# Diagonal and neighbour level of the recurrent heads as split elementwise products, and a paced recurrence

## The chip, the cores and the metric

The kernel runs on one core of one Trainium2 chip. The core has a matrix engine (TensorE, PE in the rows; its weight loads are PEld), a vector engine (DVE), an activation engine (ACT), a general engine (POOL) and a queue engine (SP), and sixteen DMA engines that move data between memory and the core. The metric is the device time of one execution in microseconds (us), lower is better.

## The reference

The program is one layer of an encoder over 512 positions of width 1024, in float32: a token mixer (eight-head grouped attention with axial rotary positions, beside four heads of a bidirectional gated recurrence), a cross-attention into 256 memory rows, and a gated feed-forward with a short convolution. The change lies in the recurrence. For one head and one direction it computes

```
b     = cumsum(log f)                                   # per key channel, f in (lb, 1)
o[t]  = sum over s <= t, channels c, of  q[t,c] * k[s,c] * exp(b[t,c] - b[s,c]) * v[s]
k     = 1 - f
```

and the backward direction is the same on the flipped sequence. Both are summed, so position t meets every position s once through a decay of one direction, and itself twice (k forward plus k backward, no decay).

## The kernel before

Everything is laid out with 128 channels on the partitions and 512 positions along the free axis. A large product in float32 is made of three matmuls on halves: each operand is split into a rounded part in the reduced type float32r and its remainder, and `mm3` (lines 277 to 280) multiplies high by high, high by low and low by high. A weight unit of 128x1024 is loaded, cast by ACT (line 222) and completed by DVE, or by ACT and a summing DMA (lines 224 to 230).

The recurrence of one head is `hgrn_core` (line 618). It has no chunks in time. It builds the 128x128 blocks of the score matrix by levels: level m (1, 2, 4, ... 64) fills the entries whose positions lie in neighbouring runs of m inside a pair of runs. `qk` holds queries and keys of both directions, already multiplied with the decays inside the runs; a level takes the keys (copied to `kc`) and the queries, multiplies them on TensorE in plain float32 (line 647, four 128x128 matmuls into one bank `ps_c`), and DVE merges the result into `diag` through a mask (line 679, `copy_predicated`). Then DVE multiplies the queries and keys with the decay to the next run in place (line 673, two instructions) and the run decays with each other (line 678). The diagonal itself is a product of its own ahead of the levels: `ksum`, the key sum of both directions (lines 628 and 629), times q (line 636), copied to `diag` by ACT (line 637). Level 1 pairs each position with its neighbour and uses copies `kc` and `qc` (line 632). Levels 128 and 256 cross the blocks (lines 654 to 666), and lines 685 to 687 apply the scores to v. Each plain float32 matmul shows as two records in the trace, so a group of four as x8.

Heads 0 to 2 run beside the input projections: `weave` (line 73) steps two generators, `mix_projections` (gate, head 1, head 2, queries of the attention, head 3, keys and values) and `cores`, and always advances the one whose done share of its given total is smaller. A projection step is six wide matmuls and counts 1.296, a level counts 1.0; the totals are 100 and 53 (`CORE_SHARE`). Head h can begin when its inputs are projected. Head 3 runs in a second `weave` beside the attention and a filler of projections. The order in which the generators emit instructions is their rank: the framework (Tile) then places each engine's instructions by that rank, by what is ready in its own plan, and by free buffers, and each engine runs its list strictly in that order. `rope_q` and `turn_q` (lines 770 to 784) rotate the attention's queries on DVE, ACT and TensorE while head 3 is projected; they read the projection's banks `ps_s` and `ps_o`, which the keys and values need next.

Temporary buffers have tags; `th` has four buffers (`kc`, `qc`, `ksum` and others), `tq` three. The bank `ps_c` has two.

Of the kernel before, what the change touches and what calls it, by code (L numbers as in the profile page):

```python
# [9 lines left out]
F32 = mybir.dt.float32  # L10
F32R = mybir.dt.float32r
# [3 lines left out]
ALU = mybir.AluOpType  # L15
# [3 lines left out]
P = 128  # L19
D = 1024  # L20
T = 512
NB = T // P
# [25 lines left out]
NEG_SCALAR = frozenset(range(9, 33))  # L48
NEG_POOL = frozenset(range(33, 42))
CORE_SHARE, ATT_LEAD = 53.0, 4.0  # L50
KEY_TURNS = {1: (0, 1), 2: (2, 3)}
WARM, SPREAD_STEP = 4, 2
LEVELS = (1, 2, 4, 8, 16, 32, 64)
# [5 lines left out]
def pat(t, off, dims):  # L59
    a = t[:]  # L60
    return bass.AP(tensor=a.tensor, offset=a.offset + off, ap=[list(a.ap[0])] + [list(d) for d in dims])
# [8 lines left out]
        return self.hi[kc // n][:, kc % n, sl], self.lo[kc // n][:, kc % n, sl]  # L70


def weave(*streams):
    live = [[g, 0.0, float(total)] for g, total in streams]
    while live:
        live.sort(key=lambda s: s[1] / s[2])
        for s in live:
            try:
                step = next(s[0])
            except StopIteration:  # L80
                live.remove(s)
                break
            if step is not None:
                s[1] += step
                break
        else:
            raise RuntimeError("no stream can go on")


def layer(tc, io, out):  # L90
    nc = tc.nc
    ctx = ExitStack()
    pool = lambda name, **k: ctx.enter_context(tc.tile_pool(name=name, **k))
    const = pool("const", bufs=1)
# [13 lines left out]
    def bank(tag):  # L108
        return ps.tile([P, 512], F32, name="ps_" + tag, tag=tag)
# [4 lines left out]
    def tmp2(shape=(P, 512), dt=F32, tag="ta"):  # L114
        return t2.tile(list(shape), dt, name="tmp2", tag=tag, bufs=TMP_BUFS[tag])
# [4 lines left out]
    def split(hi, lo, src, eng=None):  # L120
        nc.scalar.copy(hi, src)  # L121
        (eng or nc.vector).tensor_sub(lo, src, hi.bitcast(F32))  # L122
# [159 lines left out]
    def blk(b):  # L282
        return slice(b * P, (b + 1) * P)
# [153 lines left out]

    ident = const.tile([P, P], F32, name="ident")
    gcol = const.tile([P, KC], F32, name="gcol")
    ones = const.tile([P, P], F32, name="ones")  # L440
    nhalf = const.tile([P, 16], F32, name="nhalf")
    mark = const.tile([P, 1], F32, name="mark")
    warm = tmp2()
    xt = [big([P, 4, T]) for _ in range(2)]
    nc.scalar.dma_start(gcol, io["gx"])
    nc.gpsimd.memset(ones, 1.0)
    nc.vector.memset(warm[:, :256], 0.0)
    nc.gpsimd.memset(nhalf, -0.5)
# [44 lines left out]
    for j in range(4):  # L493
# [8 lines left out]
        for k in range(2):  # L502
            kc = 2 * j + k
            for a, w in ((0, wh), (0, wl), (1, wh)):
                for b in range(NB):
                    nc.tensor.matmul(v_ps[b], hT.get(kc, blk(b))[a], w[:, half(k)],
                                     start=kc == 0 and a == 0 and w is wh, stop=kc == 7 and a == 1)
# [2 lines left out]
        nc.sync.dma_start(xr[b], io["x"][blk(b), :])  # L510
    ident_r = const.tile([P, P], F32R, name="ident_r")
    nc.vector.tensor_copy(ident_r, ident)
    issued[0] = taken[0] = 4
    hold[0] = 6
    issue_ahead()
# [22 lines left out]
    masks = const.tile([P, len(LEVELS), P], U8, name="masks")  # L538
# [79 lines left out]
    def hgrn_core(h):  # L618
        while h not in heads:
            yield None  # L620
        q, qk, tt = heads[h]
        room = big([P, 2048])
        a = room[:, 0:1024].rearrange("p (s w n) -> p s w n", s=NB, w=2)
        kt = room[:, 1024:1536].rearrange("p (s n) -> p s n", s=NB)
        st = room[:, 1536:1792].rearrange("p (g n) -> p g n", g=2)
        diag = a[:, :, 0, :]
        ksum, kc, qc = [tmp2(tag="th") for _ in range(3)]
        nc.scalar.mul(ksum, qk[:, 1, 0, :], oml[:, 0, h:h + 1])
        nc.vector.scalar_tensor_tensor(out=ksum, in0=qk[:, 1, 1, :], scalar=oml[:, 1, h:h + 1], in1=ksum,
                                       op0=ALU.mult, op1=ALU.add)  # L630
        for side, to in ((1, kc), (0, qc)):
            (nc.vector.tensor_copy if (h, side) == (1, 0) else nc.scalar.copy)(
                to, pat(qk, side * 2 * T, [[2, T // 2], [T + 1, 2]]))
        o = bank("c").rearrange("p (b n) -> p b n", b=NB)
        for b in range(NB):
            nc.tensor.matmul(o[:, b, :], ksum[:, blk(b)], q[:, blk(b)], start=True, stop=True)
        nc.scalar.copy(diag, o)
        yield 1.0
        toff = 0
        for i, m in enumerate(LEVELS + (128, 256)):  # L640
            if m <= 64:
                if m > 1:
                    kc = tmp2(tag="th")
                    nc.scalar.copy(kc, pat(qk, 2 * T, [[2 * m, T // (2 * m)], [T + m, 2], [1, m]]))
                o = bank("c").rearrange("p (b n) -> p b n", b=NB)
                for b in range(NB):
                    nc.tensor.matmul(o[:, b, :], kc[:, blk(b)], qc[:, blk(b)] if m == 1 else  # L647
                                     pat(qk, b * P, [[2 * m, P // (2 * m)], [T + m, 2], [1, m]]),
                                     start=True, stop=True)
            elif m == 128:  # L650
                o = bank("c").rearrange("p (b n) -> p b n", b=NB)
                for sb in range(NB):
                    tb = sb ^ 1
                    nc.tensor.matmul(o[:, sb, :], qk[:, 1, sb % 2, blk(sb)], qk[:, 0, tb % 2, blk(tb)],
                                     start=True, stop=True)
            else:
                o = bank("c").rearrange("p (b n) -> p b n", b=NB)
                for sb in range(NB):
                    nc.tensor.transpose(o[:, sb, :], qk[:, 1, sb // 2, blk(sb)], ident)
                nc.scalar.copy(kt, o)  # L660
                yield 0.5
                o = bank("c")[:, :256].rearrange("p (g n) -> p g n", g=2)
                for sb in range(NB):
                    nc.tensor.matmul(o[:, sb // 2, :], kt[:, sb, :], v[:, sb, blk(h)],
                                     start=sb % 2 == 0, stop=sb % 2 == 1)
                nc.scalar.copy(st, o)
                yield 1.0
                break
            nblk = T // m
            npair = nblk // 2  # L670
            for s, off, gap in ((1, 1, nblk - 1), (0, nblk + 1, -(nblk + 1))):
                c = pat(qk, s * 2 * T, [[2 * m, npair], [T + m, 2], [1, m]])
                nc.vector.tensor_tensor(out=c, in0=c, in1=pat(tt, toff + off, [[2, npair], [gap, 2], [0, m]]),  # L673
                                        op=ALU.mult)
            if m < 128:
                src = tt[:, toff:toff + 2 * nblk].rearrange("p (i two) -> p two i", two=2)
                toff += 2 * nblk
                nc.vector.tensor_mul(tt[:, toff:toff + nblk], src[:, 0, :], src[:, 1, :])
                nc.vector.copy_predicated(diag, masks[:, i:i + 1, :].to_broadcast([P, NB, P]), o)
            else:  # L680
                nc.scalar.copy(a[:, :, 1, :], o)
            yield 1.0
        o = bank("c").rearrange("p (b n) -> p b n", b=NB)
        for tb in range(NB):
            nc.tensor.matmul(o[:, tb, :], a[:, tb, 0, :], v[:, tb, blk(h)], start=True, stop=False)
            nc.tensor.matmul(o[:, tb, :], a[:, tb ^ 1, 1, :], v[:, tb ^ 1, blk(h)], start=False, stop=False)
            nc.tensor.matmul(o[:, tb, :], qk[:, 0, tb // 2, blk(tb)], st[:, 1 - tb // 2, :], start=False, stop=True)
        on = tmp2((P, NB, P), tag="th")
        ss = small()
        for b in range(NB):  # L690
            nc.scalar.activation(on[:, b, :], o[:, b, :], ACT.Square, accum_out=ss[:, b:b + 1])
        r = rstd_of(ss[:, :NB], NB, P)
        yield 3.0
        while len(sg_box) < 1 + NB:
            yield None
        for b in range(NB):
            nc.vector.scalar_tensor_tensor(out=on[:, b, :], in0=o[:, b, :], scalar=r[:, b:b + 1],
                                           in1=sg_box[0][:, b, blk(h)], op0=ALU.mult, op1=ALU.mult)
        o = bank("c").rearrange("p (b n) -> p b n", b=NB)
        for b in range(NB):  # L700
            nc.tensor.transpose(o[:, b, :], on[:, b, :], ident)
        if h % 2 == 0:
            pair(mix, 2 + h // 2)
        split_scaled(*mix.get(4 + h, slice(0, T)), o.rearrange("p b n -> p (b n)"), og[:, 0:1])
        rec_done[0] += 1
        yield 0.5
# [224 lines left out]
    def attention_filler():  # L931
        kv["k"] = Act([None] * 2, [None] * 2)
        for c in range(8):
# [3 lines left out]
            for step in proj_fm(kv["m"], M, "b", put_kx(c)):  # L937
                yield step
                turned[0] = c > max(KEY_TURNS)
            for b in KEY_TURNS.get(c, ()):  # L940
# [87 lines left out]
    acts, sides, gates, last_act = [], [], {}, [None]  # L1028
# [63 lines left out]
    us = [bank(up_tags[n]) for n in range(4)]  # L1092
# [10 lines left out]
    wide = [big([P, 2, 4, 256]) for _ in range(2)]  # L1103
# [14 lines left out]
    near, far = half_t  # L1118
# [40 lines left out]
    for i in range(2, NF):  # L1159
        if i in UP_S:  # L1160
            strassen_pair(i)
        else:
            for c in range(2):
                o = next_bank()
# [182 lines left out]
```

## Time and profile before

| | |
|---|---|
| time, median of 3 runs | 816.31 us (816.14 to 816.73) |
| profiled execution, first to last instruction | 813.8 us |
| TensorE busy | 803.3 us, 99% |
| weight loads (PEld) busy | 691.0 us, 85% |
| DVE busy | 574.7 us, 71% |
| ACT busy | 482.1 us, 59% |
| POOL busy | 136.9 us, 17% |

The span of the profiled execution counts from its first to its last instruction; the runs' times hold in addition what lies around it, 2.5 us by the median. Busy time of TensorE is the union of its records, whose ends are modelled; distances from start to start are what a matmul really takes of the engine. The granted TensorE clock is full (2.4 GHz) in all forty slices of the span.

### The profile page before, as it was taken

To read this page: it belongs to the slowest core of one execution; us is meant where nothing else is said; L and a number is where in the kernel's file an instruction comes from. 1 tells how busy PE (TensorE), PEld (TensorE's weight loads), DVE (VectorE), ACT (ScalarE), POOL (GpSimd) and SP (SyncE) were. 2 spreads that over 40 slices of the span, in tenths; PEclk is the share of its full clock that TensorE was granted. 3 is DMA by queue.
4 is the path that set the end of the run, shared out by engine and by line. 5 is a ranking of instruction groups with operands and counts; after the bars stand their busy time and mean duration, and the time that the engine had idled before them with its cause. 6 is when DMAs were issued, how large, how long until landed. Compare 5 with 4: busy or idle time off the path is not lost.

```text
span 813.8 us, 11771 instructions
## 1 busy us (share of the span) xinstructions
PE 803.3 (99%) x4426; PEld 691.0 (85%) x4426; DVE 574.7 (71%) x868; ACT 482.1 (59%) x796; POOL 136.9 (17%) x213
## 2 busy tenths in 40 slices
PE   9999999999999999999999999999999999999996
PEld 7888888889998887888888898899999998888885
DVE  5456587469886865855453767987777788888765
ACT  5675757459988874644543553665555545566651
POOL 0111201053233102301010311211111111000301
PEclk9999999999999999999999999999999999999999
DMA  8685645569899753256634158776665677278852
GB/s 296 202 259 139 160 103 117 118 159 247 229 250 254 182 172 126 78 181 157 180 117 142 33 164 208 154 200 166 179 171 143 150 200 178 91 208 278 239 130 104
DMA packets 42457, 139.61 MB, mean 172 GB/s; under 512 B 5280, under 2 KB 6560, under 8 KB 42400
## 3 DMA queue, kind: packets, MB, share of 16 engines
q1 hardware_dynamic: 28944, 97.43, 35.5%
q0 software_dynamic: 12160, 38.54, 26.2%
q10 hardware_dynamic: 1296, 2.89, 1.0%
q8 instruction: 34, 0.56, 0.3%
q14 instruction: 23, 0.19, 0.1%
HBM read 135.17 MB, written 25.17 MB: 197 GB/s over the span
## 4 chain that ended last, share of the span: by engine, by line
PE 92%; DVE 3%; ACT 2%; issue 1%; POOL 1%; DMA 0%; DVEq 0%; POOLq 0%; SPq 0%; ACTq 0%
PE ps_b L279 10%; PE ps_b L280 10%; PE ps_b L278 10%; PE ps_s L278 6%; PE ps_s L280 6%; PE ps_s L279 6%; PE ps_o L278 5%; PE ps_o L279 5%; PE ps_o L280 5%; PE ps_c L278 5%; PE ps_c L280 5%; PE ps_c L279 5%; PE ps_c L647 3%; PE ps_o L893 2%; PE ps_s L872 2%; PE ps_o L882 2%
## 5 line engine op out<-in xcount | busy, mean ns | idle before, releaser
L222 ACT CAST wh<-raw 128x1024 fp32r<-128x1024 f32 x110 | 113.7, 1035 | 114.6 <-PE ps_b L279 35.3
L224 DVE TENSOR_TENSOR wl<-raw,wh 128x1024 fp32r<-128x1024 f32 (+1 forms) x77 | 92.3, 1201 | 72.2 <-ACT wh L222 72.0
L278 PE MATMUL ps_b<-big,wh 128*128 128x512 f32 (+1 forms) x344 | 122.3, 355 | 0.0
L280 PE MATMUL ps_b<-big,wl 128*128 128x512 f32 (+1 forms) x344 | 121.2, 352 | 0.0
L279 PE MATMUL ps_b<-big,wh 128*128 128x512 f32 (+1 forms) x344 | 121.2, 352 | 0.0
L280 PEld LDWEIGHTS ps_b<-big,wl 128*128 128x128 f32 x344 | 65.1, 189 | 8.5 <-DMA wl<-in_wu_dram 0.2
L278 PEld LDWEIGHTS ps_b<-big,wh 128*128 128x128 f32 x344 | 65.1, 189 | 8.3
L279 PEld LDWEIGHTS ps_b<-big,wh 128*128 128x128 f32 x344 | 65.1, 189 | 8.1
L673 DVE TENSOR_TENSOR big<-big 128x512 f32<-128x512 f32 x64 | 47.2, 755 | 9.6 <-PE ps_c L647 4.0
L278 PE MATMUL ps_s<-wh,big 128*128 128x512 f32 (+1 forms) x140 | 53.4, 383 | 0.0
L279 PE MATMUL ps_s<-wl,big 128*128 128x512 f32 (+1 forms) x140 | 53.3, 381 | 0.0
L280 PE MATMUL ps_s<-wh,big 128*128 128x512 f32 (+1 forms) x140 | 53.0, 379 | 0.0
L230 POOL DMA_DIRECT2D wl<-in_w_dram x33 | 29.3, 887 | 126.7 <-ACT wl L229 91.5
L122 DVE TENSOR_TENSOR big<-ps_o,big 128x512 fp32r<-128x512 f32 x54 | 36.9, 687 | 15.0 <-ACT big L121 13.4
L121 ACT CAST big<-ps_o 128x512 fp32r<-128x512 f32 x54 | 31.7, 588 | 18.5 <-PE ps_o L996 7.5
L278 PE MATMUL ps_s<-big,wh 128*128 128x256 f32 (+1 forms) x120 | 40.0, 334 | 0.0
L279 PE MATMUL ps_s<-big,wh 128*128 128x256 f32 (+1 forms) x120 | 40.0, 333 | 0.0
L280 PE MATMUL ps_s<-big,wl 128*128 128x256 f32 (+1 forms) x120 | 40.0, 333 | 0.0
L278 PE MATMUL ps_o<-wh,big 128*128 128x512 f32 (+1 forms) x102 | 39.2, 385 | 0.0
L279 PE MATMUL ps_c<-big,wh 128*128 128x256 f32 (+1 forms) x120 | 39.1, 326 | 0.0
L278 PE MATMUL ps_c<-big,wh 128*128 128x256 f32 (+1 forms) x120 | 39.1, 326 | 0.0
L280 PE MATMUL ps_c<-big,wl 128*128 128x256 f32 (+1 forms) x120 | 39.1, 326 | 0.0
(315 smaller groups left out, 2149.3 us busy)
## 6 DMA issues: line engine op xcount, KB each, us to landing
raw<-in_w_dram SPq DMA_DIRECT2D x91, 512.0 KB, 3.6
wl<-in_w_dram POOLq DMA_DIRECT2D x33, 512.0 KB, 7.3
sum_t<-in_wd_dram SPq DMA_DIRECT2D x20, 512.0 KB, 6.3
tmp<-in_wu_dram SPq DMA_DIRECT2D x14, 512.0 KB, 6.9
sum_t<-in_wd_dram POOLq DMA_DIRECT2D x10, 512.0 KB, 8.4
sum_t<-sum_t POOLq DMA_DIRECT2D x10, 512.0 KB, 7.5
big<-sum_t SPq DMA_DIRECT2D x10, 512.0 KB, 4.7
raw<-sum_t SPq DMA_DIRECT2D x10, 512.0 KB, 4.4
```

What stands on the lines that cost most here:

```text
L121: nc.scalar.copy(hi, src)
L122: (eng or nc.vector).tensor_sub(lo, src, hi.bitcast(F32))
L222: nc.scalar.copy(wh, raw)
L224: last_low[0] = nc.vector.tensor_sub(wl[:, :by_dma], raw[:, :by_dma], wh[:, :by_dma].bitcast(F32)).ins
L230: nc.gpsimd.dma_start(wl[:, by_dma:], source(i)[:, by_dma:], accum_op=ALU.add)
L278: nc.tensor.matmul(o, a[0], b[0], start=start, stop=False, skip_group_check=again)
L279: nc.tensor.matmul(o, a[0], b[1], start=False, stop=False, skip_group_check=again)
L280: last_mm[0] = nc.tensor.matmul(o, a[1], b[0], start=False, stop=stop, skip_group_check=again).ins
L647: nc.tensor.matmul(o[:, b, :], kc[:, blk(b)], qc[:, blk(b)] if m == 1 else pat(qk, b * P, [[2 * m, P // (2 * m)], [T + m, 2], [1, m]]), st ...
L673: nc.vector.tensor_tensor(out=c, in0=c, in1=pat(tt, toff + off, [[2, npair], [gap, 2], [0, m]]), op=ALU.mult)
L872: nc.tensor.matmul(s, qT[h // 4][:, h % 4, blk(qb)], kT[:, 2 * (h // 4) + c, :], start=c == 0, stop=c == 1)
L882: nc.tensor.transpose(o[:, c, :], e[:, 0, blk(c)], ident)
```

## The change

For heads 0 to 2 (`wide`), the diagonal and level 1 are no longer matrix products. DVE multiplies neighbours elementwise (each query with the neighbour's key of the right direction) and `ksum` with q, and interleaves them into two planes of 128x512, `near`: in plane 0 an even column holds the diagonal and an odd column the pair, in plane 1 the other way round. Both planes are split into high and low parts, and four float32r matmuls of 128x512 with a stationary pattern of ones and zeros in alternate columns (`parity`) sum the channels: row s of the result receives plane s mod 2. ACT copies the result to `diag`; entries that are neither diagonal nor pair are overwritten by the later levels. Head 3 keeps the former way, with all its copies on ACT.

In both weaves the recurrence is now paced by a clock that counts what all streams have emitted: after each level it waits until 2.0 of other work has been emitted (`CORE_STEP`), before the pattern products 6.0 (`CORE_WIDE`), before head 3's diagonal 3.0 (`CORE_FIRST`); when nobody else can go on, the wait is dropped. `ones` moves to a temporary buffer, and `parity` takes its place among the constants.

```diff
+CORE_FIRST, CORE_STEP, CORE_WIDE = 3.0, 2.0, 6.0
+clock, stuck = [0.0], [False]
+def pace(us):
+    end = clock[0] + us
+    while clock[0] < end and not stuck[0]:
+        yield None
 def weave(*streams):
...
             if step is not None:
                 s[1] += step
+                clock[0] += step
+                stuck[0] = False
                 break
         else:
-            raise RuntimeError("no stream can go on")
+            if stuck[0]:
+                raise RuntimeError("no stream can go on")
+            stuck[0] = True
...
-    ones = const.tile([P, P], F32, name="ones")
+    parity = const.tile([P, P + 2], F32R, name="parity")
...
+    ones = tmp2((P, P), tag="tq")
...
+    for i in range(2):
+        nc.vector.memset(parity.rearrange("p (i two) -> p i two", two=2)[:, :, i].bitcast(F32), 1.0 - i)
...
-        ksum, kc, qc = [tmp2(tag="th") for _ in range(3)]
+        wide = h < 3
+        near = room[:, 1024:2048]
+        ksum = tmp2(tag="th")
         nc.scalar.mul(ksum, qk[:, 1, 0, :], oml[:, 0, h:h + 1])
+        if wide:
+            nc.vector.tensor_tensor(out=pat(near, T, [[2, T // 2], [1 - T, 2]]), in0=pat(qk, 0, [[2, T // 2], [T + 1, 2]]),
+                                    in1=pat(qk, 3 * T + 1, [[2, T // 2], [-(T + 1), 2]]), op=ALU.mult)
         nc.vector.scalar_tensor_tensor(out=ksum, in0=qk[:, 1, 1, :], scalar=oml[:, 1, h:h + 1], in1=ksum,
                                        op0=ALU.mult, op1=ALU.add)
-        for side, to in ((1, kc), (0, qc)):
-            (nc.vector.tensor_copy if (h, side) == (1, 0) else nc.scalar.copy)(
-                to, pat(qk, side * 2 * T, [[2, T // 2], [T + 1, 2]]))
-        o = bank("c").rearrange("p (b n) -> p b n", b=NB)
-        for b in range(NB):
-            nc.tensor.matmul(o[:, b, :], ksum[:, blk(b)], q[:, blk(b)], start=True, stop=True)
-        nc.scalar.copy(diag, o)
-        yield 1.0
+        if wide:
+            pairs = lambda t: t.rearrange("p (i two) -> p i two", two=2)
+            nc.vector.tensor_tensor(out=pat(near, 0, [[2, T // 2], [T + 1, 2]]), in0=pairs(ksum), in1=pairs(q),
+                                    op=ALU.mult)
+            sides = [[tmp2(dt=F32R, tag="th") for _ in range(2)] for _ in range(2)]
+            for n in range(2):
+                split(*sides[n], near[:, n * T:n * T + T])
+        else:
...
+            yield from pace(CORE_FIRST)
...
-            if m <= 64:
+            if m == 1 and wide:
+                pass
+            elif m <= 64:
...
-                nc.vector.copy_predicated(diag, masks[:, i:i + 1, :].to_broadcast([P, NB, P]), o)
+                if m == 1 and wide:
+                    yield from pace(CORE_WIDE)
+                    o = bank("c")
+                    for n in range(2):
+                        for k in range(2):
+                            nc.tensor.matmul(o, parity[:, n:n + P], sides[n][k], start=n + k == 0, stop=n + k == 2)
+                    nc.scalar.copy(diag, o.rearrange("p (b n) -> p b n", b=NB))
+                else:
+                    nc.vector.copy_predicated(diag, masks[:, i:i + 1, :].to_broadcast([P, NB, P]), o)
             else:
                 nc.scalar.copy(a[:, :, 1, :], o)
             yield 1.0
+            yield from pace(CORE_STEP)
```

## Rows read from the trace of the kernel before

**Rows 1.** The page, first part: each engine's busy time, share, instructions.
```profile
PE 803.3 (99%) x4426; PEld 691.0 (85%) x4426; DVE 574.7 (71%) x868; ACT 482.1 (59%) x796; POOL 136.9 (17%) x213
```

**Rows 2.** Waits of TensorE: total us, times, longest us.
```profile
PE ps_c L647 <- DVE big L673: 0.7, 1, 0.7
...
PE ps_c L647 <- ACT tmp L644: 0.5, 1, 0.5
```

**Rows 3.** Timeline of TensorE, head 0: start, duration, line, tiles, count.
```profile
44.79 0.39 PE L278 MATMUL ps_s<-wh,big 128*128 128x512 f32 x1
...
50.45 0.39 PE L279 MATMUL ps_s<-wl,big 128*128 128x512 f32 x1
...
54.31 1.05 PE L636 MATMUL ps_c<-tmp,tmp 128*128 128x128 f32 x8
55.11 0.48 PE L278 MATMUL ps_o<-wh,big 128*128 128x512 f32 x1
55.43 1.05 PE L647 MATMUL ps_c<-tmp,tmp 128*128 128x128 f32 x8
56.24 0.48 PE L279 MATMUL ps_o<-wl,big 128*128 128x512 f32 x1
```

**Rows 4.** Timeline of head 1 on TensorE, DVE and ACT.
```profile
99.21 1.04 ACT L229 ACTIVATE wl<-wh 128x1024 fp32r<-128x1024 f32 x1
99.34 0.75 DVE L607 SCALAR_TENSOR_TENSOR big<-big,oml,tmp 128x512 f32<-128x512 f32 x1
99.47 1.13 PE L636 MATMUL ps_c<-tmp,tmp 128*128 128x128 f32 x8
100.35 0.48 PE L279 MATMUL ps_b<-big,wh 128*128 128x512 f32 x1
...
100.90 0.40 PE L278 MATMUL ps_b<-big,wh 128*128 128x512 f32 x1
...
101.04 2.15 DVE L673 TENSOR_TENSOR big<-big 128x512 f32<-128x512 f32 x2
101.25 1.13 PE L647 MATMUL ps_c<-tmp,tmp 128*128 128x128 f32 x8
102.14 0.47 PE L279 MATMUL ps_b<-big,wh 128*128 128x512 f32 x1
...
103.33 1.20 PE L647 MATMUL ps_c<-big,tmp 128*128 128x128 f32 x8 [0.72 <-DVE big L673]
```

**Rows 5.** Timeline of TensorE, first groups of head 3.
```profile
195.43 1.06 PE L636 MATMUL ps_c<-tmp,tmp 128*128 128x128 f32 x8
...
207.46 1.16 PE L647 MATMUL ps_c<-big,tmp 128*128 128x128 f32 x8 [0.52 <-ACT tmp L644]
```

**Rows 6.** Single lines: shortest, median, longest duration in ns.
```profile
L679 DVE COPY_PREDICATED big<-masks,ps_c x28: 706/730/751, 56.6 to 236.9; 128x512 f32<-128x512 uint8 x28
...
L121 ACT CAST tmp<-tmp x4: 604/620/627, 177.1 to 191.4; 128x512 fp32r<-128x512 f32 x4
...
L122 DVE TENSOR_TENSOR tmp<-tmp,tmp x4: 681/686/694, 177.9 to 192.3; 128x512 fp32r<-128x512 f32 x4
...
L647 PEld LDWEIGHTS ps_c<-tmp,tmp x32: 187/192/193, 55.2 to 199.9; 128*128 128x128 f32 x32
```

**Rows 7.** Windows: length, busy us (instructions) of each engine, clock, DMA share, GB/s.
```profile
core 0: us, PE busy (x) PEld busy (x) DVE busy (x) ACT busy (x) POOL busy (x), PEclk, DMA share, GB/s
...
165.00:180.00 15.00, 15.00 (x76) 12.60 (x75) 10.50 (x20) 8.93 (x19) 7.61 (x10) 1.00 0.61 131
180.00:196.00 16.00, 16.00 (x137) 15.58 (x136) 15.43 (x28) 14.54 (x25) 6.38 (x8) 1.00 0.91 255
```

**Rows 8.** DVE by line, 130 to 166 us: busy us, mean ns, idle before.
```profile
L673 DVE TENSOR_TENSOR big<-big 128x512 f32<-128x512 f32 x16 | 11.6, 745 | 5.3 <-PE ps_c L654 2.3 <-PE ps_c L647 1.9 <-ACT tmp L644 1.1
L679 DVE COPY_PREDICATED big<-masks,ps_c 128x512 f32<-128x512 uint8 x7 | 5.1, 729 | 0.0
```

**Rows 9.** Timeline, hand-over of the last query bank to keys and values.
```profile
187.41 0.68 DVE L736 TENSOR_TENSOR tmp<-ps_o,big 128x512 f32<-128x512 f32 x1
...
188.38 0.28 PE L278 MATMUL ps_o<-wh,big 128*128 128x256 f32 x1
```

More of the change, by code (lines that the diff above doesn't have):

```diff
@@ L626, in hgrn_core @@
         diag = a[:, :, 0, :]
-        ksum, kc, qc = [tmp2(tag="th") for _ in range(3)]
+        wide = h < 3
+        near = room[:, 1024:2048]
+        ksum = tmp2(tag="th")
         nc.scalar.mul(ksum, qk[:, 1, 0, :], oml[:, 0, h:h + 1])
+        if wide:
+            nc.vector.tensor_tensor(out=pat(near, T, [[2, T // 2], [1 - T, 2]]), in0=pat(qk, 0, [[2, T // 2], [T + 1, 2]]),
+                                    in1=pat(qk, 3 * T + 1, [[2, T // 2], [-(T + 1), 2]]), op=ALU.mult)
         nc.vector.scalar_tensor_tensor(out=ksum, in0=qk[:, 1, 1, :], scalar=oml[:, 1, h:h + 1], in1=ksum,
                                        op0=ALU.mult, op1=ALU.add)
-        for side, to in ((1, kc), (0, qc)):
-            (nc.vector.tensor_copy if (h, side) == (1, 0) else nc.scalar.copy)(
-                to, pat(qk, side * 2 * T, [[2, T // 2], [T + 1, 2]]))
-        o = bank("c").rearrange("p (b n) -> p b n", b=NB)
-        for b in range(NB):
-            nc.tensor.matmul(o[:, b, :], ksum[:, blk(b)], q[:, blk(b)], start=True, stop=True)
-        nc.scalar.copy(diag, o)
-        yield 1.0
+        if wide:
[6 more added lines that the diff above has]
+        else:
+            kc, qc = [tmp2(tag="th") for _ in range(2)]
+            for side, to in ((1, kc), (0, qc)):
+                nc.scalar.copy(to, pat(qk, side * 2 * T, [[2, T // 2], [T + 1, 2]]))
+            yield from pace(CORE_FIRST)
+            o = bank("c").rearrange("p (b n) -> p b n", b=NB)
+            for b in range(NB):
+                nc.tensor.matmul(o[:, b, :], ksum[:, blk(b)], q[:, blk(b)], start=True, stop=True)
+            nc.scalar.copy(diag, o)
+            yield 1.0
         toff = 0
         for i, m in enumerate(LEVELS + (128, 256)):
-            if m <= 64:
+            if m == 1 and wide:
+                pass
+            elif m <= 64:
                 if m > 1:
```

## The prediction

> **What bounds the kernel now.** I read the page's busy times first, then TensorE's waits, then its timeline from start to start, and last the busy times of short windows. The page gives TensorE 803.3 of 813.8 us [rows 1]: the reader is to see that an instruction removed from it shortens the kernel, unless something else comes to the fore. The waits say how little is left to gain by order alone: in the level products (line 647) TensorE waited 0.7 us once for DVE and 0.5 us once for ACT [rows 2]. The first is in head 1, at 103.33 [rows 4]. The second is in head 3, at 207.46 [rows 5]. Because ends of matmuls are modelled, I price TensorE by starts. A wide float32r product of 512 columns takes 0.227 us: from 44.79 to 50.45 lie 25 of them, 5.66 us [rows 3]. A float32 group of four 128x128 products takes 0.80 us to the next start in head 0 (54.31 to 55.11), and the wide matmul after it stands 0.32 instead of 0.227 from its successor, so a change of kind costs 0.09 more [rows 3]. The clock is full in these windows [rows 7], as in the whole span.
>
> **TensorE's part of the change.** Each of three heads loses two groups (diagonal, level 1). In head 0: 0.80 + 0.09 + 0.81 + 0.09 = 1.79 us [rows 3]. In head 1: 0.88 to 100.35, 0.89 from 101.25 to 102.14, 0.12 for the matmul at 100.90 that stands 0.35 from the group, and two changes of 0.09: 2.07 [rows 4]. The mean is 1.93, for three heads 5.8 us. Each gains four wide float32r products: 12 x 0.227 = 2.7 us. The net is -3.1. Bounds: 3 x 1.61 (bare groups) - 2.7 = 2.1 below, 3 x 2.07 - 2.7 = 3.5 above. The pattern products have no row of their own; the nearest is the ordinary split product, of the same shape and type, and its weight load lies under the product before it, so I take its 0.227.
>
> The Trainium skill's "TensorE: Matmul & The Clock Gate", section "Back-to-back issue gap", gives about 131 ns for a product of 512 columns in a sustained stream; by that the added products would be an estimated 1.6 us and the net -4.2. The trace does not agree: its stream keeps 0.227 [rows 3], and the row decides.
>
> **DVE and ACT.** Per wide head DVE gains the neighbour product and the product with q, both on stride-2 operands like the level-1 decay product, 2.15 / 2 = 1.08 each [rows 4], and two remainders of 0.69 [rows 6]; it loses one masked merge of 0.73 [rows 6]: +2.8 us, 8.4 in all. ACT loses two strided copies and gains two casts of 0.62 [rows 6]: I cost that at nothing or a small gain. No DMA is added or removed. The two fills of the pattern (65 columns each) and the move of `ones` to a temporary buffer fall before the first head, with wide products queued on TensorE; they cost nothing, and less than a microsecond of DVE if uncovered. What hides the 8.4 us on DVE is TensorE's own stream, as long as DVE has room: in 165 to 180 it is busy 10.5 of 15, in 180 to 196 15.4 of 16 [rows 7].
>
> **The order.** I worked the two weaves through by their yields. Before, a level came after 1.0 x 100 / 53 = 1.9 of projection on the average, but with none between as long as the recurrence lagged; that is head 1, which waits for its inputs and then ranks its first levels one right behind the other. The wait at 103.33 stands in that run: DVE's two level-1 decays (2.15 us from 101.04) had to end before the level-2 product [rows 4]. After, 2.0 means two projection steps (2 x 1.296), 12 matmuls or 2.7 us, before each level, and 6.0 means five steps, 30 matmuls or 6.8 us, ahead of the pattern products. So that wait goes: -0.7 us. What is late next is the pattern product itself. Its chain in head 1 starts when line 607 ends, 100.09 [rows 4]: 1.08 + 1.08 + 0.62 + 0.69 + 0.69 brings 104.3, or 106.4 if DVE puts the level-1 decays in front. TensorE gets there five steps after the place of the first group: 99.47 + 6.8 = 106.3. It fits, barely. Queued behind a late pattern product stand all projections in TensorE's list, and nobody else. The wait that it can cost is unknown; below it is nothing (the chain as added up), above 0.72 in each of three heads, 2.2, as the one wait shown. A second source of waits is that the end of a head (the transposes, the state, the output, the norm) has no pace and ranks in one lump, since a paced head lags its share; there TensorE has the projections as cover, and each hand-over that is not covered costs up to the 0.5 of the ACT wait [rows 2]. I take 1.0 us for new waits together, between the bounds, as the chain fits by the sum. In the second weave the former pace, (46 + 52) / 22 = 4.5 per level, is above 2.0 already, so the step costs nothing there; a later first product of head 3 is hidden by the filler's projections, and head 3's old wait of 0.5 I leave where it is.
>
> **Sum.** -3.1 - 0.7 + 1.0 = -2.8 us on the span of 813.8, so 811.0; with the 2.5 us that lie around the span by the median of 816.3, the forecast is 813.5 us.
>
> **Rivals.** *DVE becomes the bound while head 3 is projected (slower).* A paced head takes 21 projection steps from its first product to level 256. Head 2 then ranks its levels in steps 55 to 71 of 76, where before it ranked them in 41 to 57. Steps 57 to 76 are head 3's projection and the keys and values, and there the rotation of the queries runs on DVE. What moves there: 11.6 us of decays and 5.1 of merges [rows 8] without level 1 (2.2 and 0.7), 13.8 us. The stretch 165 to 196 now holds 25.9 us of DVE work in 31 [rows 7]; with seven level groups of 0.96 TensorE stretches it to 38, DVE wants 39.7. That alone is 2.0 us short; if the 4.5 us that DVE stands idle in its first half stay out of use, because the rotation waits for its banks, it is 6.5, and the time is 816.3 - 3.8 + 6.5 = 819.0. It decides from 3.8 us of new waits on. For it: the last query bank is released at 188.09 (187.41 + 0.68) and the keys and values take it at 188.38 [rows 9], so this hand-over is already just in time. Against it: TensorE is busy 16.00 of 16 us while DVE is at 15.43 [rows 7], and the planner can bring other projections forward.
>
> *The pattern products wait as much as is saved (no change).* If in each head one weight cast or completion of ACT (1.04 at 99.21 [rows 4]) comes in front of the casts of the two planes, the chain ends about 1 us later than TensorE: 3 x 1.04 = 3.1, and the time is 816.3 - 3.1 - 0.7 + 3.1 = 815.6. Against it: the planner ranks these casts ahead of later weights.
>
> *Weight loads set TensorE's pace (faster still).* Removed are 48 loads of 0.192, 9.2 us [rows 6], added 12 of the like, 2.3: 6.9 less, and with -0.7 + 1.0 the time is 809.7. Against it: eight loads of 0.192 would be 1.5 us, but a group of eight stands 0.80 from its successor [rows 3], so loads overlap. The Trainium skill's "Perfetto Trace Analysis", section "Identifying the Most-Contended Engine", would have TensorE judged by its loads' busy share and not by that of its products; by that rule it has 15% left [rows 1], and no row here shows the loads as the limit.
>
> **How the numbers follow.** Forecast 0.66, no change 0.17, DVE bound 0.14, loads 0.03. A measurement of this kernel can tell about 0.2%, 1.6 us, from no change. The likeliest case alone reaches from 816.3 - 3.5 - 0.7 - 0.2 (a little of head 3's wait) = 811.9 to 816.3 - 2.1 - 0.7 + 2.2 = 815.7. The range takes the low end from there, holds the no-change case, and goes into the DVE case to 816.8, where its waits are 4.3 us. Faster by over 0.2%: 0.66 + 0.03 = 0.69; within 0.2%: 0.17; slower by over 0.2%: 0.14.
>
> **What would show it.** Right: twelve pattern products spaced 0.23 us, no float32 groups at lines of the diagonal and level 1 in heads 0 to 2, head 3's first product about 3 us earlier than 195.43 [rows 5], levels spaced by 12 wide matmuls, no wait at a level-2 product, DVE busy about 583 us. Wrong: a wait of over 0.7 us at the pattern products (the chain), or TensorE idle between the end of the queries' projection and head 3 with DVE above 95% (the DVE bound); then the order and not the removed products decides.

## The result, and the profile after the change

| | before | after |
|---|---|---|
| median of 6 runs each, us | 816.22 (815.76 to 816.73) | 818.77 (818.15 to 819.14) |
| ratio, 95% interval | 1 | 1.003 (1.0019 to 1.0041) |
| profiled span, us | 813.8 | 816.4 |

The kernel became slower by 0.3%, where faster by 0.3% was forecast. The first part of the page of the kernel after the change answers to [rows 1]:

```profile
PE 801.7 (98%) x4390; PEld 688.9 (84%) x4390; DVE 582.7 (71%) x878; ACT 481.5 (59%) x797; POOL 137.4 (17%) x213
```

DVE gained 8.0 us (forecast 8.4) and TensorE lost 36 instructions, as the change says: 48 small products out, 12 wide ones in. The page gives TensorE less work in a longer span, so the loss must stand among its waits. This is the start of that view after the change (us in total, times, longest us); the row of `parity` belongs to the first microseconds, where the kernel before waits as long.

```profile
PE ps_c L743 <- DVE tmp L739: 3.3, 3, 1.2
PE ps_b L481 <- DVE parity L529: 1.3, 1, 1.3
PE ps_s L292 <- DVE big L136: 1.1, 1, 1.1
PE ps_c L717 <- DVE tmp L136: 0.6, 1, 0.6
PE ps_o L935 <- DVE big L136: 0.2, 1, 0.2
PE ps_c L717 <- ACT tmp L135: 0.2, 1, 0.2
```

Neither row of [rows 2] is there any more: the waits at level products went. In their place stand three kinds of wait: the transposes that close a head (line 743, behind the norm in line 739; before, lines 701 and 697), a query projection (line 292) and the pattern products (line 717).

**The closing transposes.** Before, the end of head 0 ran like this (timeline of the kernel before; the first row is the last output product, the last row the transposes, of which this view ends before the fourth):

```profile
79.48 0.39 PE L687 MATMUL ps_c<-big 128*128 128x128 f32 x2
...
81.46 1.04 POOL L297 TENSOR_TENSOR small<-small,nhalf 128x4 f32<-128x4 f32 x1
...
82.53 1.12 DVE L697 SCALAR_TENSOR_TENSOR tmp<-ps_c,small,big 128x128 f32<-128x128 f32 x4 [3.83 <-POOL small L297]
...
85.17 0.49 PE L701 MATMUL ps_c<-ident,tmp 128*128 128x128 f32 x3
```

After the change (timeline; the first row is again the last output product):

```profile
87.60 0.39 PE L729 MATMUL ps_c<-big 128*128 128x128 f32 x2
...
88.95 0.22 ACT L733 ACTIVATION_READ_ACCUMULATOR tmp<-ps_c 128x1 f32 x1
...
89.55 1.04 POOL L311 TENSOR_TENSOR small<-small,nhalf 128x4 f32<-128x4 f32 x1
...
90.63 1.13 DVE L739 SCALAR_TENSOR_TENSOR tmp<-ps_c,small,big 128x128 f32<-128x128 f32 x4 [8.68 <-POOL small L311]
...
91.12 0.30 PE L743 MATMUL ps_c<-ident,tmp 128*128 128x128 f32 x1 [1.04 <-DVE tmp L739]
```

The reader is to see that the chain is as long as it was: squares on ACT, the power on POOL (1.04 us), the norm on DVE. Before, DVE's norm stood 3.05 us behind the last output product, after it 3.03. What changed is the place of the transposes in TensorE's list. Before, 5.7 us of TensorE's work lay between the start of the last output product and theirs, more than the chain needs. After, it is 2.5 us, and then TensorE waits 1.04 for the norm. DVE itself had been idle for 8.68 us ahead of the norm, so it was not the cause. The same happens at 146.96 (1.04) and 199.80 (1.22), where DVE had been idle for 6.88 and 5.03.

**The pattern products.** In head 0 they stand in the stream as forecast, 0.23 us to the next start (timeline of TensorE):

```profile
56.00 0.39 PE L717 MATMUL ps_c<-tmp,parity 128*128 128x512 f32 x1
56.23 0.40 PE L293 MATMUL ps_s<-wl,big 128*128 128x512 f32 x1
...
56.70 0.40 PE L717 MATMUL ps_c<-tmp,parity 128*128 128x512 f32 x1
```

In head 1 the chain is late (all engines):

```profile
103.34 1.15 DVE L655 TENSOR_TENSOR big<-tmp,tmp 128x512 f32<-128x512 f32 x1
...
104.31 1.19 DVE L706 TENSOR_TENSOR big<-big 128x512 f32<-128x512 f32 x1
...
105.19 0.50 PE L717 MATMUL ps_c<-tmp,parity 128*128 128x512 f32 x1 [0.23 <-ACT tmp L135]
105.33 0.69 DVE L594 TENSOR_TENSOR tmp<-ps_b,big 128x512 f32<-128x512 f32 x1
105.93 0.41 DVE L711 TENSOR_TENSOR big<-big 128x256 f32<-128x256 f32 x1
...
106.26 0.68 DVE L136 TENSOR_TENSOR tmp<-big,tmp 128x512 fp32r<-128x512 f32 x1
106.59 0.60 ACT L135 CAST tmp<-big 128x512 fp32r<-128x512 f32 x1
...
106.99 0.76 PE L717 MATMUL ps_c<-tmp,parity 128*128 128x512 f32 x2 [0.60 <-DVE tmp L136]
```

Level 1's decays (lines 706, 711) and head 2's inputs (line 594) come in front of the remainder on DVE. By starts the twelve pattern products take 3.56 us, 0.84 more than 12 x 0.227.

**The query projection.** The transposes of the memory's turn end at 120. ACT casts their result, DVE makes the remainder, and the first query product waits for it (all engines):

```profile
119.44 0.60 PE L331 MATMUL ps_o<-ident,big 128*128 128x128 f32 x4
...
119.75 0.80 ACT L622 ACTIVATE big<-big,lb,oml 128x512 f32<-128x512 f32 x1
119.79 0.68 DVE L706 TENSOR_TENSOR big<-big 128x512 f32<-128x512 f32 x1
119.88 1.06 PE L680 MATMUL ps_c<-big,tmp 128*128 128x128 f32 x8
120.45 0.56 ACT L135 CAST big<-ps_s 128x512 fp32r<-128x512 f32 x1
120.58 0.75 DVE L624 SCALAR_TENSOR_TENSOR big<-big,oml,tmp 128x512 f32<-128x512 f32 x1
...
121.25 0.68 DVE L136 TENSOR_TENSOR big<-ps_s,big 128x512 fp32r<-128x512 f32 x1
...
121.99 0.50 PE L292 MATMUL ps_s<-wh,big 128*128 128x512 f32 x1 [1.05 <-DVE big L136]
```

The first of the four transposed banks was full at about 118.7, but its cast starts at 120.45: ACT first copies the keys of head 1's next level (118.17) and prepares head 2's inputs (lines 620 to 622, from 118.70). On DVE a level's decay (line 706) and head 2's inputs (line 624) stand ahead of the remainder. Before, the same turn came at 126.88, and its first cast ran ahead of head 2's inputs (all engines, kernel before):

```profile
127.81 0.58 ACT L121 CAST big<-ps_s 128x512 fp32r<-128x512 f32 x1
128.28 0.63 ACT L603 ACTIVATE big<-tmp 128x512 f32<-128x512 f32 x1
...
129.16 0.50 PE L278 MATMUL ps_s<-wh,big 128*128 128x512 f32 x1
```

So two things changed: head 1's levels, which before were over by then, now lie across this turn, and head 2's inputs come ahead of its casts. Which of them costs how much was not tried apart. The slot from 119.88 to 121.99 is 2.11, 1.30 above a bare group.

**The sum by starts.** Between 28 and 310 us the groups of the diagonal fall from 3.30 to 0.81 us and those of the levels from 23.92 to 22.04, which holds the 1.30 just named: 2.49 + 1.88 + 1.30 = 5.7 us fewer (forecast 5.8). The bare pattern products add 2.7, so the products give -3.0 (forecast -3.1). The old waits give -0.7 - 0.5. Against that stand the closing transposes with 3.9, of which 3.3 is waiting (in head 1 lie four wide products, 0.91, between 145.53 and 148.13, and four transposes, which together with the change of kind took 0.45 in head 0 before; that leaves 1.24, and in the same way 1.25 in head 0 and 1.38 in head 2), the pattern waits with 0.8 and the query projection with 1.3. Two waits of 0.2 for weights and turns come behind 470 us. That is -3.0 - 1.2 + 6.0 + 0.4 = +2.2; the trace has +2.5 at the end, and 0.3 has no row.

### The profile page after: what moved, and what is told of

It is laid out like the page before. It is cut to its first block, busy times and chain, and to the rows that moved or that the text cites. A ratio compares the mean times of both kernels' runs of the same rounds, so it can differ in the third digit from the quotient of the medians.

```text
span 816.4 us, 11689 instructions
## 1 busy us (share of the span) xinstructions
PE 801.7 (98%) x4390; PEld 688.9 (84%) x4390; DVE 582.7 (71%) x878; ACT 481.5 (59%) x797; POOL 137.4 (17%) x213
```

## The experiments

Each ratio is to the kernel before, run on the same chip, with its 95% interval; an offset says how much later than in the trace of before TensorE starts its 300th matmul of the first line of `mm3` (there at 307 us). After the change that offset is +2.1. With each edit the framework orders all lists anew, so two runs can differ in more than the edit. No run that computes the whole layer was faster than the kernel before.

**Which half costs? e2 (products without pace) and e3 (pace without products).**

```
e2:  def pace(us):
+        return
e3:  -wide = h < 3
     +wide = False        # and head 1's copy on DVE, as before
```

> The changed kernel with the pace switched off: heads 0 to 2 keep the elementwise products and the pattern products, the order follows the shares 100 to 53 alone. Theory (head ends): the norm gets its distance back from the share, so the 3.3 us at the closing transposes go; the pattern products rank right behind their chain and wait up to 1 us in each head, and the wait at a level-2 product comes back (0.7): 816.2 - 3.1 + 0 to 3 = 813.1 to 816.1. Rival (DVE bound): the gain comes from head 2's levels that leave the stretch of the rotation, 814 too, but then the closing transposes of heads 0 and 1 still wait.

> The pace alone: all four heads keep the matrix products of diagonal and level 1, with pace 3.0 ahead of the diagonal and 2.0 after each level. Theory (head ends): the closing transposes of heads 0 to 2 wait 3.3 us together, the wait of 0.7 in head 1 goes: 816.2 + 3.3 - 0.7 = 818.8. Rival (DVE bound): DVE has 8.4 us less to do than in the changed kernel, so most of the loss goes: 816 to 817, without waits at the transposes of heads 0 and 1.

Measured: e2 816.67 us, 1.0004 (0.9995 to 1.0012); e3 820.88 us, 1.0056 (1.0042 to 1.0069). The pace costs 4.6 us by itself, and 2.1 on top of the products; the products alone give nothing. Waits of e3 (traced at 822.69 us):

```profile
PE ps_c L744 <- DVE tmp L740: 3.0, 3, 1.0
PE ps_s L915 <- ACT big L801: 1.8, 1, 1.8
...
PE ps_b L294 <- DMA wl<-in_wu_dram: 1.1, 1, 1.1
```

Three closing waits come with the pace, also without the new products. The 2 us above the expected 818.8 go with a wait of 1.8 at attention's first scores, behind which TensorE's clock falls (last section), and with one of 1.1 for a weight. Waits of e2:

```profile
PE ps_c L718 <- DVE tmp L137: 1.1, 1, 1.1
PE ps_c L744 <- DVE tmp L740: 1.0, 1, 1.0
PE ps_s L915 <- ACT big L801: 0.7, 1, 0.7
PE ps_c L718 <- ACT tmp L136: 0.5, 1, 0.5
```

Without pace the pattern products come too early for their chain (1.6 us), and the closing of one head (1.0) and the first scores of attention (0.7) wait as well. So a closing wait can come without the pace too, but one and not three.

**What are the closing waits worth? e7.** The norm multiplies by a constant column and not by the reciprocal root, so it no longer waits for ACT's squares and POOL's power; the recurrence's output is not normalised.

```
-  ... scalar=r[:, b:b + 1],
+  ... scalar=nhalf[:, b:b + 1],
```

> The changed kernel with the order as it is, but the norm at the end of a head reads a constant column instead of its own reciprocal root, so the chain from the output products to the closing transposes no longer goes through ACT's squares and POOL's power (they still run, nobody waits for them); the recurrence's output is not normalised. Theory: the waits at the transposes come from POOL's power instruction (1.04 us), which the plan of the order holds for shorter; without it in the chain at most 0.3 us of wait are left in each head, 818.8 - 2.5 = 816.3. Rival (DVE's queue is late, whatever the chain): the waits stay at 1.0 to 1.2 each.

Measured 815.45 us, 0.9999 (0.999 to 1.0007), offset -0.5: 0.31% better than the changed kernel, 2.5 us. Its longest waits behind the first microseconds:

```profile
PE ps_s L292 <- DVE big L136: 1.1, 1, 1.1
PE ps_c L717 <- DVE tmp L136: 0.6, 1, 0.6
```

No closing wait is left; the query projection's and the pattern's are, unchanged, and two of 0.5 and 0.6 came in behind 200 us. The 2.5 us are the whole loss against before, and most of what the closings take by starts.

**Can they be covered? e1 and e11.** e1 puts 4.0 us of the others' work between a head's output products and its norm; e11 does it for heads 0 to 2 and halves the step in head 2, so that this head does not end later.

```
e1:             yield 3.0
            +   yield from pace(4.0)
e11:        -   yield from pace(CORE_STEP)
            +   yield from pace(1.0 if h == 2 else CORE_STEP)
                ...
            +   yield from pace(4.0 if h < 3 else 0.0)
```

> The changed kernel with one more pace, 4.0 of other work between a head's output products and its norm (behind the yield of 3.0). Theory (head ends): the changed kernel ranks the end of a head in one lump, and TensorE meets the closing transposes of heads 0 to 2 before the norm is done, 3 waits of together 3.3 us; they go, and the time falls from 818.8 to about 815.5. Rival (DVE bound while head 3 is projected): the waits are DVE's backlog and move elsewhere; the time stays within 0.5 us of 818.8, and head 2 gets worse as its end moves later.

> The changed kernel with 4.0 of other work between output products and norm for heads 0 to 2, and, to keep head 2's end where the changed kernel has it (step 71 of 76), a step pace of 1.0 instead of 2.0 in head 2. Theory: the closing waits (3.3) go as they did with the constant column, and no collision with head 3 takes their place: 815.5. If the earlier run with the end pace lost by its pace and not by head 2's lateness, it stays at 818 to 819.

Measured: e1 819.1 us, 1.0034 (1.0022 to 1.0046). In its traced execution (820.7 us) the closing waits of heads 0 and 1 are gone but head 2's (1.43) and two of head 3's groups (0.38, 0.94) wait close together; TensorE's clock falls (windows of e1: length, busy of PE, PEld, DVE, ACT, POOL, granted clock, DMA):

```profile
201.00:203.00 2.00, 0.83 (x3) 0.41 (x3) 1.72 (x8) 1.97 (x4) 1.13 (x3) 1.00 0.81 162
203.00:205.00 2.00, 1.49 (x10) 1.16 (x10) 2.00 (x5) 1.53 (x2) 0.75 (x1) 1.00 0.57 170
205.00:207.00 2.00, 1.06 (x7) 0.87 (x6) 2.00 (x4) 1.56 (x4) 0.18 (x1) 0.51 1.02 285
207.00:209.00 2.00, 2.00 (x11) 2.00 (x11) 1.13 (x3) 2.00 (x6) 0.00 (x0) 0.50 1.00 197
```

e11 817.03 us, 1.001 (1.0002 to 1.0019): no closing wait, 0.2% better than the changed kernel. It keeps the query wait (1.1), the pattern's grow from 0.8 to 1.4, and others come in at the turns of the queries (line 823, 0.6) and of the keys (line 800, 1.2 together). So the closing waits can be had back: of the 2.5 us of e7 1.7 arrive, and the rest is taken by the new ones.

**The pattern's chain. e4** gives it nine units of lead, not six.

```
-CORE_FIRST, CORE_STEP, CORE_WIDE = 3.0, 2.0, 6.0
+CORE_FIRST, CORE_STEP, CORE_WIDE = 3.0, 2.0, 9.0
```

> The changed kernel with 9.0 instead of 6.0 of other work ahead of the pattern products (CORE_WIDE). Theory: the waits at the pattern products (about 1.4 us over heads 1 and 2) go, the closing transposes still wait 3.3 us: 817.4. Rival (DVE bound): each head ends two projection steps later and head 2's levels fall later still; 819 to 820.

Measured 818.48 us, 1.0029 (1.0018 to 1.0041). The pattern waits go, all of them, and the time stays. In the traced execution (817.41 us) heads 2 and 3 come later still, with a closing wait of 1.42 and 0.72 at head 3's first product, behind which the clock is 0.53, 0.50 and 0.50 in the windows of 1 us from 203 to 206.

**Other paces. e5** (step 1.0, wide 8.0, end 4.0) **and e8** (step 0.0, wide 8.0, end 4.0; the end for heads 0 to 2).

> The changed kernel with another pace: 1.0 after each level (one projection step instead of two), 8.0 ahead of the pattern products (seven steps instead of five), and 4.0 more between output products and norm for heads 0 to 2. By the yields head 2 then ends its levels at step 63 and its norm at 67 of 76, where the changed kernel has 71 and the kernel before 54 and 57. Theory (the rank of the paced steps, not the products, loses the time): no wait at closing transposes, none at the pattern products, no collision with head 3: 816.3 - 3.1 + 0.7 = about 813.9. Rival (the elementwise products load DVE and ACT so that TensorE's saving does not arrive): 816 to 818, with waits on DVE elsewhere.

> The changed kernel without the pace after each level, with 8.0 ahead of the pattern products and 4.0 ahead of the norm: the levels follow the shares as in the kernel before, head 2 ends its levels at step 50 and its norm at 61. Theory (rank of the paced steps): the removed products come through and only waits at level-2 products as in the kernel before are left, 816.3 - 3.1 + 0 to 1.5 = 813.2 to 814.7. Rival (DVE and ACT loaded by the elementwise products): 816 or more, with several waits on DVE or ACT at the level products, since a level now follows the other at 2.0 us.

Measured: e5 819.39 us, 1.0045 (1.0033 to 1.0057): neither closing nor pattern waits, but 2.5 us in one at the query projection, and 3.9 in six others between 187 and 234 us, the longest (1.3) for a weight. That is above both of its expectations. The clock falls behind the first (windows of e5):

```profile
120.00:122.00 2.00, 0.29 (x1) 0.29 (x2) 1.70 (x3) 2.00 (x5) 0.00 (x0) 1.00 0.80 123
122.00:124.00 2.00, 2.00 (x7) 1.58 (x7) 2.00 (x5) 1.87 (x6) 0.00 (x0) 0.64 0.72 141
124.00:126.00 2.00, 2.00 (x7) 1.61 (x7) 1.43 (x4) 0.54 (x1) 0.00 (x0) 0.51 0.00 0
```

e8 816.37 us, 1.0008 (1.0 to 1.0017): as before, within what can be told. It waits at head 1's last products (lines 687, 692 and 697, 2.0 us between 122 and 126), at a closing (0.9) and at a level of head 3 (0.5).

**The rival with DVE. e6** leaves head 2 without the step, so that it ends before the queries' rotation, as it used to.

```
-            yield from pace(CORE_STEP)
+            yield from pace(CORE_STEP if h != 2 else 0.0)
```

> The changed kernel with the step pace 2.0 for heads 0 and 1 alone; head 2 keeps the 6.0 ahead of its pattern products and is not paced after them, so its levels rank one right behind the other in step 55. Theory (head 2 too late, DVE-bound stretch of the rotation): head 2's end leaves the keys and values, its wait at the transposes (1.2) and the ones in the attention's first scores go: 816.5 to 817.5. If lateness of head 2 costs nothing, the time stays at 818.8, or gets worse as its levels rank ahead of the rotation.

Measured 819.33 us, 1.0043 (1.003 to 1.0056): no better. In the changed kernel DVE is full in one stretch of those that answer to [rows 7], and there TensorE is as well:

```profile
165.00:180.00 15.00, 15.00 (x104) 13.64 (x103) 14.95 (x25) 8.11 (x11) 9.88 (x10) 1.00 0.81 205
180.00:196.00 16.00, 16.00 (x140) 15.73 (x139) 12.83 (x28) 11.55 (x21) 1.72 (x3) 1.00 0.51 121
```

So the rival falls. Its 819.0 is nearer to the result than the forecast, but by chance: the waits are at closings ahead of which DVE stood idle.

**What are the removed products worth? e9** is the kernel before without the diagonal and level-1 products of heads 0 to 2, with nothing in their place: the diagonal block is a copy of the keys' sum, and level 1 merges the copied queries, so the scores of these heads are not computed. The edit is shortened here; head 3 keeps its products.

```
-        for b in range(NB): nc.tensor.matmul(o[:, b, :], ksum[:, blk(b)], q[:, blk(b)], ...)
-        nc.scalar.copy(diag, o)
+        if h < 3: nc.scalar.copy(diag, ksum.rearrange("p (b n) -> p b n", b=NB))
...
+            if m == 1 and h < 3: o = qc.rearrange("p (b n) -> p b n", b=NB)
```

> The kernel before, in its own order, without the diagonal and the level-1 products of heads 0 to 2 (six float32 groups left out; diag and the level-1 merge read other buffers instead, nothing else is changed, so the scores of these heads are not the reference's). It prices what is removed: by the starts in the trace 1.93 us a group pair, 5.8 us for three heads, so 810.2 if the price is right and no wait takes its place. Rival (part of the price was cover for waits on DVE and ACT): less than 4 us faster, with new waits at the level products.

Measured 812.89 us, 0.9966 (0.9954 to 0.9978): -3.35 us by the medians of that chip, not -5.8. Waits of e9:

```profile
PE ps_c L706 <- DVE tmp L702: 1.9, 1, 1.9
...
PE ps_c L652 <- DVE big L678: 1.0, 1, 1.0
```

The first is a closing, where the kernel before has none; the second is the wait of [rows 2], up from 0.7. With two more of 0.2 the first weave (28 to 165 us) now waits 3.3 where it waited 0.7: TensorE comes 2.6 us sooner to chains that did not get shorter.

**Fewer wide heads, without pace: e10** (heads 0 and 2) **and e12** (head 0).

```
-        wide = h < 3
+        wide = h in (0, 2)      # e12: h == 0
```

`pace` returns at once, as in e2, and a head that is not wide has its copies as before.

> No pace, elementwise products for heads 0 and 2 alone; head 1, whose inputs arrive last and whose pattern product waited 1.1 us without the pace, keeps the matrix products. Theory: two thirds of the product saving (2 x 1.0) and the old wait of 0.7 in head 1: 816.0 - 2.0 = 814, a version faster than both. Rival (what the products free is lost in waits whatever the head): 816.

> No pace, elementwise products for head 0 alone, whose pattern products did not wait in any run. Theory: 1.0 us less than before and nothing else: 815. Rival: no difference from before, 816.

Measured: e10 818.05 us, 1.0031 (1.0017 to 1.0045); e12 817.56 us, 1.0017 (1.0008 to 1.0026). e10 is worse than all three heads without pace; e12 is by the medians, but its interval touches that of e2. Both show a closing wait of 1.04 in head 1 (at 126.9 and 126.3) and 0.81 at attention's first scores, which the kernel before does not have. e12's products are worth an estimated -1.0 (a third of -3.0), its listed waits behind the first 28 us are 1.5 us above those of before, and 0.9 of its +1.4 has no row. That is open: I did not find why the planner's order suits head 0 alone so badly.

## Why the prediction was wrong

**Right.** The products' own saving on TensorE (-3.0 for -3.1), at the 0.227 us of the split products; the level-2 wait, which went; DVE's 8 us; and that DVE would not become the bound.

**The step that failed** is "I take 1.0 us for new waits together". They measured 6.0 us by starts. Of its two sources the pattern's chain stayed inside its bounds, 0.8 between nothing and 2.2, though its sum did not hold in head 1: it left out the keys' sum (line 651, 0.72 us), TensorE came to the pattern products at 105.0 and not at 106.3, and the first remainder ended at 106.94 and not between 104.3 and 106.4. The other source was named, "the end of a head (the transposes, the state, the output, the norm) has no pace and ranks in one lump", but mis-sized. I priced an uncovered hand-over at the 0.5 of an ACT wait [rows 2]; it cost 1.24 to 1.38 in each of three heads. The trace of before held the better number: 3.05 us from the last output product to the norm, and the 5.7 us by which the transposes stood behind. The chain up to the first transpose takes 3.5, so it needs that much work in front of the transposes, and a lump leaves only the planner's choice. e7 shows that these waits are worth 2.5 us, e3 that the pace brings them, and e11 that they go when the end is paced too.

**A wait that I did not name** is the query projection, 1.3 us by starts. The prediction looked at heads 1 and 2 as sequences of their own; it did not ask what the stretched head 1 would now lie across, which is the memory's turn at 118 to 122. That the stretching is the cause is in part argued: without a pace between the levels e2 and e8 have no wait at this product, but e10 and e12 have one of 0.5, and e3, with the pace alone, has no more. Head 3's first product was forecast 3 us earlier than in [rows 5]; it came at 201.95, 6.5 later, as the heads ahead of it had been stretched and waited (without the pace, in e2, it comes at 196.38). The levels do stand 12 wide products apart, as said (64.45, 68.08, 71.71: 3.63 us each), but in head 0 there had been no wait to cure.

**A gain that depends on what follows.** The sum took each removed group at its price on TensorE. e9 shows that with the six groups simply gone 2.6 us of the 5.8 turn into waits, and e2 that the replaced products alone give nothing. The saving is there by starts; it buys an earlier arrival at chains on ACT, POOL and DVE.

**The rivals.** That DVE bounds head 3's projection falls by e6 and by the windows. That the pattern products wait as much as is saved holds only without pace, in part (1.6 us in e2). Weight loads were not seen to set the pace: fewer loads (688.9 us, from 691.0) went with a longer span.

## What to carry to other kernels

On an engine that is 98% busy, the slack of every hand-over is a number that can be read beforehand: how long the chain is (here 3.5 us) and how much work stands in front of its consumer (5.7 before the change, 2.5 after). Work that is removed or moved shortens the second and leaves the first, so list these pairs for all hand-overs that the change shifts, and take the excess as the price. And when the steps of a sequence are spaced, look at its end: spacing the steps alone cured a wait of 0.7 us at one level product and brought three at closings. Spacing the end as well is not yet a gain. It gave back 1.7 us in e11, but in e1 and e5 the waits moved to other hand-overs, and the time was no better.

## What was not expected of the hardware

In four of the experiments the granted clock fell to 0.50 or 0.51, the lower level of 1.2 GHz, though before and after the change it is full as long as TensorE works. Each time TensorE had waited just before: 2.5 us at once in e5 (busy 0.29 of 2 us), 1.42 and 0.72 in e4, 1.43 and 0.38 in e1 (and 0.94 more at the low clock), 1.82 in e3, where the windows of 4 us from 212 show 0.93 and 0.65. From the windows of e5 the price behind the wait is an estimated (1 - 0.64) x 2 + (1 - 0.51) x 2 = 1.7 us; for e1, with 0.63 and 0.52 in the windows of 4 us from 204, it is at most 3.4. The Trainium skill's "TensorE: Matmul & The Clock Gate", section "HAM oscillation — how this bites in real kernels", describes a kernel whose waits for DMA throttle the engine, so that the work behind them starts cold; the traces of these four agree, though here the waits are for ACT and DVE. Not every such wait does it. In e9 TensorE waited 1.91 us at once (busy 0.57 of the 2 us from 126), and in e8 it was busy 2.3 of the 4 us from 122; the clock stayed full in both. Behind the waits of the changed kernel no window of 4 us shows a lower clock either. What tells these cases apart is open.

POOL's power takes 1.04 us for four columns and 0.55 to 0.96 for one (kernel before). It is the longest single instruction of the closing chain ahead of the norm, and POOL's 17% on the page does not show it.
